# Two gates of the latent branch handed to the latent attention's filler, with that branch's products two gates behind

## The chip, the cores and the metric

The kernel runs on one core of a Trainium2 chip. A core has five engines that run their own queues in order and wait for each other through semaphores: TensorE (PE, with its weight loads PEld), VectorE (DVE), ScalarE (ACT), GpSimd (POOL) and SyncE (SP), whose queue issues the weight transfers here. The metric is the device time of one execution in microseconds (us), the median over several runs. One execution is taken by the hardware profiler, and all rows in the text come from it.

## What is computed

Two layers of an encoder trunk on 512 tokens of width 1024. In each layer, after one combined input projection of the normalised input, three branches are computed, each is projected to the model width, weighted by a sigmoid gate per token and channel, summed, and projected once more; a gated feed-forward with a short convolution follows. Cut to what matters here:

```
o_mla  = mla_branch(c_q, c_kv, k_rope, ...)      # 8 heads, latent attention
o_gqa  = gqa_branch(gq, gk, gv, ...)             # 8 heads, grouped queries
o_pool = pool_branch(pool_in, ...)
gates  = sigmoid(gate_logits)                    # 3 x 1024 channels, columns of h @ w_in
merged = gates[0] * (o_mla  @ w_branch_mla) + gates[1] * (o_gqa @ w_branch_gqa) \
       + gates[2] * (o_pool @ w_branch_pool)
x = x + merged @ w_out
x = x + (silu(u_gate) * u_val) @ ffn_w_down      # u: up-projection and width-3 convolution
```

The gate logits depend on the normalised input alone, the products `o @ w_branch` on the finished branch.

## The kernel before, in words

All work on TensorE is done with operands split into a high and a low part: `mm3` (L347) issues three matmuls of up to 512 columns for one product of 128 rows. Weights come from memory in order of use as one long stream of pieces; a piece is split into `wh` (ACT, L208) and `wl` (POOL or DVE, L215) shortly before its use, two pieces ahead, into four pairs of buffers.

The order of instructions on every engine is written while the kernel is built: the program keeps a clock of its own (`Clock`, L117) with a cost for each operation, and puts the follow-up steps of a matmul (`chain`, L167) into the engines' queues when that clock reaches them. On the chip the engines run these fixed queues and wait for semaphores.

Each of the three branches ends in `gates` (L804), a generator that yields unit by unit. A unit is one `mm3`, three matmuls. For each of the eight blocks m of 128 output channels there are two pieces of work:

- `gate(m)` (L806, called "g" in the order): 8 units that sum the gate logits over the eight blocks of the input; then `logits` on DVE multiplies them with the row norm into a tile `gt`, and ACT applies the tanh that makes the sigmoid.
- `branch(m)` (L819, "b"): 4 units that multiply the four head pairs of the branch (tiles `oh`, `ol`) with the branch weight; then `product` on DVE multiplies with the gate, `add` adds into the merged tile `XM`, and for the last of the three branches the sum is split into `mgh` (ACT) and `mgl` (DVE) and the residual is fetched back into `XM` by a transfer on SP.

`_order` (L57) says how the two are interleaved: g0 g1 b0 g2 b1 ... g7 b6 b7, so that b(m) comes one gate behind g(m). The same function orders the weight stream and its packing.

A `Filler` (L94) hands out such units one at a time. `attention` (L1026) lays its own steps on a plan of positions and before each step takes units from its filler: up to a target that rises evenly to the filler's total, and beyond it, up to 35 units, while the build-time clock says that the step would wait. A head of the latent attention consists of the transposes of queries and keys, four `s_max` products with a row maximum on DVE, `m_row` (one small matmul whose result DVE writes into four rows of `qa`), and for four key blocks k: `probs` (three matmuls into `ps_ST`, then on ACT the exponential and the copy `ph`, then on DVE the rest `pl`), `av_hi` (two matmuls that need `ph`) and `av_lo` (one that needs `pl`). After the last of a pair of heads `o_out` (L1192) copies sums and values (ACT, `osum` and `oraw`), takes four reciprocals (DVE, L235), multiplies and splits into `oh` and `ol`; for the last pair multiplication and `ol` are on DVE, for the others on POOL.

Branch 2 (pool) fills the grouped attention, branch 1 (grouped) fills the latent attention with 100 units, and branch 0 (latent) runs by itself behind the latent attention, since its products need that attention's heads. Then the output projection begins, whose every sum runs over all eight merged blocks.

Of the kernel before, what the change touches and what calls it, by code (L numbers as in the profile page):

```python
# [21 lines left out]
KC = D // P  # L22
# [34 lines left out]
def _order(br):  # L57


    r = []  # L60
    for m in range(KC + 1):
        r += [(k, pos.index(m)) for k, b, pos in EXTRA if b == br and m in pos]
        if m < KC:
            r.append(("g", m))
        if m > 0:
            r.append(("b", m - 1))
    return r


# [4 lines left out]
def _widths():  # L74

    r = [384] * KC + [T] * 8 + [T] * KC + [288] * 4 + [T] + [288] * 4
    for br in (2, 1, 0):
        for k, _ in _order(br):
            r += WIDTHS[k]
    return r + [T] * (2 * KC) + [T] * (4 * FC) + [T] * (2 * FC)  # L80
# [36 lines left out]
class Clock:  # L117
# [37 lines left out]
    def done(self, *key):  # L155
        self.ready[key] = self.fin + self.SEM

    def need(self, *keys):
        for k in keys:
            while k not in self.ready:  # L160
                self.pop()
            self.to(self.ready[k])
# [4 lines left out]
    def chain(self, *steps, after=0.2):  # L167

        def go(n, source=None):
            if n == len(steps):  # L170
                return
            keys, fn = steps[n] if isinstance(steps[n], tuple) else ((), steps[n])
            late = [self.ready.get(k, self.now + 0.5) for k in keys]
            if late and max(late) > self.now:
                self.at(max(late) - self.now, lambda: go(n))
                return
            self.fin, self.source, self.last = self.now, source, None
            fn()
            source, self.source = self.last, None
            self.at(max(0.0, self.fin - self.now), lambda: go(n + 1, source))  # L180
        self.at(after, lambda: go(0))
# [61 lines left out]
def trunk(ctx: ExitStack, tc: tile.TileContext, x, w, prm, gb, cst, out):  # L243
# [17 lines left out]
    def slot(name, dt=F32):  # L261
        uid[0] += 1
        t = sp.tile([P, SLOT], dt, tag="s", name=f"{name}_{uid[0]}")
        return t
# [9 lines left out]
    def ps(tag):  # L274
        while not banks[tag]:
            ck.pop()
        ck.to(heapq.heappop(banks[tag]))
        uid[0] += 1
        t = pp.tile([P, T], F32, tag=tag, name=f"ps_{tag}_{uid[0]}", bufs=nbank[tag])
        return t  # L280

    def free(tag):
        heapq.heappush(banks[tag], ck.fin + ck.SEM)
# [48 lines left out]
    def wnext():  # L332
        j = st["use"]
        w_ahead(j + st["la"] if j > LA else j)
        st["use"] += 1
        need(("w", j))
        return halves.pop(j)
# [9 lines left out]
    def mm3(o, lh, ll, rh, rl, start, stop):  # L347
        mm(o, lh, rh, start, False)
        mm(o, lh, rl, False, False)
        mm(o, ll, rh, False, stop)  # L350
# [19 lines left out]
    def split(hi, lo, src, scale=None, eng=None):  # L370

        steps = []
        if scale is None:
            steps.append(lambda: A.activation(hi, src, AF.Copy))
            steps.append(lambda: (eng or V).tensor_tensor(lo, src, f(hi), ALU.subtract))
        else:
            steps.append(lambda: A.activation(hi, src, AF.Copy, scale=scale))
            steps.append(lambda: V.scalar_tensor_tensor(lo, src, scale, f(hi), ALU.mult, ALU.subtract))
        return steps
# [120 lines left out]
    def layer(l, sq, xsrc):  # L500
# [48 lines left out]
        def feat_major(acc, gen):  # L549

            for kc in range(KC):
                if kc:
                    yield
                if kc % 4 == 0:
                    wh, wl = wnext()
                need(("H", gen, kc))
                ws = slice((kc % 4) * P, (kc % 4) * P + P)
                mm3(acc, wh[:, ws], wl[:, ws], HH[:, kc, :], HL[:, kc, :], kc == 0, kc == KC - 1)
# [245 lines left out]
        def gates(br, okey, odst, mode):  # L804
            hold = {}

            def gate(m):
                tag = "AV" if br == 2 and m < 2 else "acc"
                acc = ps(tag)
                yield from feat_major(acc, G1)  # L810
                t = hold[m] = slot("gt")

                def logits():
                    V.tensor_tensor(t[:, :T], acc, nrm["rbc"][:, :T], ALU.mult)
                    free(tag)

                chain(([("rbc", G1)], logits), lambda: A.activation(t[:, :T], t[:, :T], AF.Tanh, scale=0.5))

            def branch(m):  # L819
                acc = ps("acc")  # L820
                wh, wl = wnext()
                for kc in range(4):
                    if kc:
                        yield
                    need((okey, l, kc))
                    ws = slice(kc * P, kc * P + P)
                    oh, ol = odst[kc]
                    mm3(acc, wh[:, ws], wl[:, ws], oh[:, :T], ol[:, :T], kc == 0, kc == 3)
                t = hold.pop(m)

                def product():
                    dst = XM[:, m, :] if mode == "first" else t[:, :T]
                    V.scalar_tensor_tensor(dst, t[:, :T], 1.0, acc, ALU.add, ALU.mult)
                    free("acc")

                def add():
                    (V if mode == "last" else G).tensor_tensor(XM[:, m, :], XM[:, m, :], t[:, :T], ALU.add)

                def fin():
                    SY.dma_start(XM[:, m, :], xsrc[m])  # L840
                    done("mrg", l, m)

                if mode == "first":
                    chain(product)
                elif mode == "add":
                    chain(product, add)
                else:
                    mh, ml = slot("mgh", F32R), slot("mgl", F32R)
                    merged[m] = (mh, ml)
                    chain(product, add, *split(mh[:, :T], ml[:, :T], XM[:, m, :]), fin)  # L850

            extra = None
            for k, m in _order(br):
                if k in mla_make:
                    extra = mla_make[k](m)
                    continue
                work = branch(m) if k == "b" else gate(m)
                more = True
                while more:
                    if extra:  # L860
                        if next(extra, END) is END:
                            extra = None
                        yield
                    more = next(work, END) is not END
                    yield
# [395 lines left out]
        ogqa, omla = {}, {}  # L1261

        def units(br):
            return sum(UNITS[k] for k, _ in _order(br))
# [6 lines left out]
        while not ck.has(*[("gqn", l, b) for b in range(4)]) and fa.step():  # L1271
            pass
        attention("gqa", fa, "og", ogqa)
        fb = Filler(gates(1, "og", ogqa, "add"), units(1))
        fb.upto(PRE_B)
        while not ck.has(("mq", l, 0)) and fb.step():
            pass
        attention("mla", fb, "om", omla)
        Filler(gates(0, "om", omla, "last"), units(0)).finish()


        sq = slot("sq")
# [69 lines left out]
        last = l == L - 1  # L1352
# [45 lines left out]
    for l in range(L):  # L1398
        sq = layer(l, sq, x if l == 0 else xsp)
# [133 lines left out]
```

## Time and profile before

| what | us |
|---|---|
| median of 3 runs (lowest, highest) | 1684.97 (1683.23, 1685.66) |
| the profiled execution, its own time | 1685.89 |
| span of that execution, first to last instruction | 1684.1 |
| outside the span, by these two | 1.8 |

Stages of the first layer, by busy time of the engines in windows of the span (us):

| stage | window | PE | DVE | ACT | POOL |
|---|---|---|---|---|---|
| input projections, pool branch, norms | 0 to 118 | 104.43 | 89.47 | 54.51 | 54.79 |
| grouped attention, branch 2 as filler | 118 to 211 | 89.28 | 69.84 | 64.35 | 44.25 |
| latent attention, branch 1 as filler | 211 to 366 | 152.35 | 106.74 | 85.46 | 73.32 |
| branch 0 | 366 to 440 | 74.00 | 28.25 | 27.10 | 34.85 |
| output projection | 440 to 483 | 43.00 | 10.87 | 18.59 | 28.17 |
| feed-forward, up | 483 to 771 | 288.00 | 174.40 | 122.30 | 173.71 |
| feed-forward, down | 771 to 895 | 124.00 | 38.54 | 41.00 | 61.59 |

The second layer repeats this about 833 us later. The boundaries are rounded. A row of the timeline gives start and duration in us, engine, line, operation, output and inputs, shapes and count; in brackets the idle time of the engine just before it and what ended it. Matmuls are pipelined and their ends are modelled, so the time that a stretch of TensorE takes is read from the starts.

### The profile page before, as it was taken

How to read it: one execution, taken by the hardware profiler on the slowest of the kernel's cores; microseconds unless marked ns; L12 is line 12 of the kernel's file. 1: busy time of each engine (PE TensorE's matmuls, PEld its weight loads, DVE VectorE, ACT ScalarE, POOL GpSimd, SP SyncE). 2: the span in 40 equal slices, each digit the busy share in tenths (PEclk: the TensorE clock that was granted, in tenths of full speed). 3: DMA queues.
4: the chain of work that ended last, by engine and by line, in shares of the span. 5: the costliest groups of instructions: out<-in, count | busy, mean ns of one | idle time of the engine just before them, and what ended most of it. 6: DMA issues, size and time to landing. Idle time of an engine off the chain costs nothing.

```text
span 1684.1 us, 20306 instructions
## 1 busy us (share of the span) xinstructions
PE 1649.9 (98%) x7360; PEld 1332.9 (79%) x7360; DVE 952.3 (57%) x1542; ACT 773.0 (46%) x1364; POOL 885.1 (53%) x746
## 2 busy tenths in 40 slices
PE   8989999999999999999999999999999999999999
PEld 7777777778888888888887777777788888888887
DVE  7777767653356666630157777677533666766100
ACT  5356755553444444432334567455434444444221
POOL 4432763444566656655544427643446665666543
PEclk9999999999999999999999999999999999999999
DMA  5221121114323333233332211111133233232331
GB/s 173 79 85 50 51 72 52 39 53 127 110 87 99 90 99 96 91 109 116 99 108 79 82 45 60 60 51 51 59 128 102 87 100 100 89 100 88 112 119 56
DMA packets 44596, 145.40 MB, mean 86 GB/s; under 512 B 5072, under 2 KB 6352, under 8 KB 44496
## 3 DMA queue, kind: packets, MB, share of 16 engines
q1 hardware_dynamic: 44352, 144.10, 27.1%
q8 instruction: 58, 0.95, 0.3%
q14 instruction: 42, 0.34, 0.1%
q10 hardware_dynamic: 144, 0.01, 0.0%
HBM read 139.90 MB, written 4.19 MB: 86 GB/s over the span
## 4 chain that ended last, share of the span: by engine, by line
PE 88%; issue 5%; DVE 2%; ACT 2%; POOL 2%; DMA 1%; SPq 0%; POOLq 0%; ACTq 0%; DVEq 0%
PE ps_acc L340 40%; PE ps_ST L340 22%; PE ps_AV L340 22%; PE ps_S L340 2%; POOL wl L215 2%; PE ps_mi L344 1%; PE ps_mi L340 1%; ACT ps_ST L208 0%; DVE tabg L215 0%; ACT ph L208 0%; DMA raw<-w 0%; DMA prm<-prm 0%; DVE wl L215 0%; ACT qa L208 0%; ACT wh L208 0%
## 5 line engine op out<-in xcount | busy, mean ns | idle before, releaser
L215 POOL TENSOR_TENSOR wl<-raw,wh 128x512 fp32r<-128x512 f32 (+1 forms) x514 | 678.2, 1329 | 664.6 <-ACT wh L208 562.7
L208 ACT ACTIVATE wh<-raw 128x512 fp32r<-128x512 f32 (+3 forms) x522 | 314.8, 609 | 188.7 <-PE ps_ST L340 89.7
L219 DVE SCALAR_TENSOR_TENSOR a<-u,prm,a 128x512 f32<-128x512 f32 x176 | 240.1, 1365 | 79.5 <-ACT a L208 76.1
L340 PE MATMUL ps_acc<-HH,wh 128*128 128x512 f32 x592 | 234.6, 396 | 4.5 <-DVE XM L219 4.3
L340 PE MATMUL ps_acc<-HH,wl 128*128 128x512 f32 x592 | 233.9, 395 | 1.2 <-POOL wl L215 1.2
L340 PE MATMUL ps_acc<-HL,wh 128*128 128x512 f32 x592 | 233.7, 395 | 0.0
L340 PEld LDWEIGHTS ps_acc<-HH,wh 128*128 128x128 f32 x592 | 111.6, 189 | 31.2 <-ACT wh L208 5.7
L340 PEld LDWEIGHTS ps_acc<-HH,wl 128*128 128x128 f32 x592 | 111.5, 188 | 28.4 <-POOL wl L215 2.1
L340 PEld LDWEIGHTS ps_acc<-HL,wh 128*128 128x128 f32 x592 | 111.7, 189 | 25.2
L208 ACT ACTIVATE ps_ST<-ps_ST 128x512 f32<-128x512 f32 x128 | 74.5, 582 | 121.6 <-PE ps_ST L340 121.2
L340 PE MATMUL ps_AV<-HH,wh 128*128 128x512 f32 x288 | 113.9, 395 | 0.0
L340 PE MATMUL ps_AV<-HH,wl 128*128 128x512 f32 x288 | 113.7, 395 | 0.0
L340 PE MATMUL ps_AV<-HL,wh 128*128 128x512 f32 x288 | 113.7, 395 | 0.0
L223 DVE TENSOR_REDUCE nm<-ps_S 128x1 fp32r<-128x512 f32 x128 | 87.6, 684 | 44.4 <-PE ps_S L340 43.6
L215 POOL TENSOR_TENSOR al<-a,ah 128x512 fp32r<-128x512 f32 x44 | 58.2, 1323 | 84.8 <-ACT ah L208 56.5
L215 DVE TENSOR_TENSOR pl<-ps_ST,ph 128x512 fp32r<-128x512 f32 x128 | 87.1, 681 | 27.6 <-ACT ph L208 27.0
L340 PE MATMUL ps_ST<-HH,wh 128*128 128x512 f32 x240 | 94.9, 395 | 0.0
L340 PE MATMUL ps_ST<-HL,wh 128*128 128x512 f32 x240 | 94.8, 395 | 0.0
L340 PE MATMUL ps_ST<-HH,wl 128*128 128x512 f32 x240 | 94.7, 395 | 0.0
L208 ACT ACTIVATE a<-u,prm 128x512 f32<-128x512 f32 x88 | 71.9, 817 | 30.7 <-DVE u L215 30.7
L208 ACT ACTIVATE ah<-a 128x512 fp32r<-128x512 f32 x44 | 27.8, 632 | 116.3 <-DVE u L239 110.9
L208 ACT ACTIVATE a<-a 128x512 f32<-128x512 f32 x44 | 27.9, 633 | 114.0 <-DVE u L239 114.0
(343 smaller groups left out, 3542.3 us busy)
## 6 DMA issues: line engine op xcount, KB each, us to landing
raw<-w SPq DMA_DIRECT2D x228, 512.0 KB, 3.5
raw<-w SPq DMA_DIRECT2D x13, 384.0 KB, 3.1
XM<-x SPq DMA_DIRECT2D x16, 256.0 KB, 3.9
raw<-w SPq DMA_DIRECT2D x6, 448.0 KB, 3.3
xsp<-XM SPq DMA_DIRECT2D x8, 256.0 KB, 2.0
XM<-xsp SPq DMA_DIRECT2D x8, 256.0 KB, 3.1
out<-XM SPq DMA_DIRECT2D x8, 256.0 KB, 2.5
raw<-w SPq DMA_DIRECT2D x4, 432.0 KB, 3.2
```

What stands on the lines that cost most here:

```text
L208: return self.eng.activation(out, in_, func, **k)
L215: return self.eng.tensor_tensor(out, *a)
L219: return self.eng.scalar_tensor_tensor(out, *a)
L223: return self.eng.tensor_reduce(out, in_, *a, **k)
L340: PE.matmul(o, lhsT=lhsT, rhs=rhs, start=start, stop=stop)
L344: PE.transpose(o, src, ident)
```

## The change

`_order` gets a lag: two for branch 0, one for the others. For branch 0 the order becomes g0 g1 g2 b0 g3 b1 ... g7 b5 b6 b7. The filler of the latent attention becomes a generator that first hands out all 100 units of branch 1 and then 16 units of branch 0, its gates g0 and g1; its total is 116. What is left of branch 0 runs behind the attention, from wherever the generator stands.

```diff
-    r = []
-    for m in range(KC + 1):
+    r, lag = [], 2 if br == 0 else 1
+    for m in range(KC + lag):
         r += [(k, pos.index(m)) for k, b, pos in EXTRA if b == br and m in pos]
         if m < KC:
             r.append(("g", m))
-        if m > 0:
-            r.append(("b", m - 1))
+        if m >= lag:
+            r.append(("b", m - lag))
     return r
...
         attention("gqa", fa, "og", ogqa)
-        fb = Filler(gates(1, "og", ogqa, "add"), units(1))
+        fc = Filler(gates(0, "om", omla, "last"), units(0))
+
+        def beside():
+
+            yield from gates(1, "og", ogqa, "add")
+            for _ in range(2 * KC):
+                fc.step()
+                yield
+
+        fb = Filler(beside(), units(1) + 2 * KC)
         fb.upto(PRE_B)
         while not ck.has(("mq", l, 0)) and fb.step():
             pass
         attention("mla", fb, "om", omla)
-        Filler(gates(0, "om", omla, "last"), units(0)).finish()
+        fc.finish()
```

No instruction is added or removed; the same matmuls, splits and transfers stand in another order. On TensorE the order differs from the fifth head of the latent attention on to the end of branch 0, in each layer. Written with g and b for a filler unit, P for the three matmuls of `probs`, A for the two of `av_hi`, a for the one of `av_lo` and M for `m_row`, the end of the latent attention reads, from the last head's M on:

```
before: M Aa P Aa P Aa P Aa P Aa Aa g x16 b x4 g x8 b x4 ... g x8 b x8
after:  M Aa g P Aa P g Aa g P g A g a P g x2 Aa g x3 Aa g x11 b x4 g x8 ... g x8 b x12
```

## Prediction

> **What bounds the kernel now.** I read the page's head first, then the busy time by stage, then TensorE's waits in the stage that the change touches, then its timeline there.
>
> ```profile
> span 1684.1 us, 20306 instructions
> ...
> PE 1649.9 (98%) x7360; PEld 1332.9 (79%) x7360; DVE 952.3 (57%) x1542; ACT 773.0 (46%) x1364; POOL 885.1 (53%) x746
> ```
>
> TensorE is busy 98% of the span, so only idle time on TensorE can be won. The windows say where it is: the end of the latent attention, branch 0 alone, the feed-forward, and a short stretch of the second layer.
>
> ```profile
> 355.00:366.00 11.00, 9.40 (x35) 5.17 (x34) 4.62 (x7) 6.77 (x12) 5.54 (x6) 1.00 0.00 0
> 366.00:440.00 74.00, 74.00 (x321) 60.03 (x321) 28.25 (x39) 27.10 (x47) 34.85 (x27) 1.00 0.39 122
> 483.00:895.00 412.00, 412.00 (x1809) 335.80 (x1807) 212.95 (x351) 163.30 (x278) 235.30 (x175) 1.00 0.32 98
> 950.00:954.00 4.00, 3.71 (x13) 3.00 (x12) 1.53 (x3) 2.73 (x6) 0.36 (x1) 0.59 0.44 131
> ```
>
> Branch 0 has no idle time: 74.00 us for 321 matmuls, 0.231 us from start to start. The last 11 us of the attention hold 35 matmuls, which at that pitch are 8.1 us. The waits in that window:
>
> ```profile
> PE ps_AV L340 <- ACT ph L208: 1.3, 3, 0.6
> PE ps_ST L340 <- DVE qa L215: 0.3, 1, 0.3
> ```
>
> The last head has run out of filler, so TensorE stands still while ACT and DVE make `qa`, `ph` and `pl`. The starts show more than the waits:
>
> ```profile
> 355.55 0.22 PE L340 MATMUL ps_mi<-idr,nm 128*4 128x128 f32 x1
> ...
> 356.36 0.40 PE L340 MATMUL ps_ST<-qa,kl 96*128 96x512 f32 x1
> ...
> 357.30 0.47 PE L340 MATMUL ps_ST<-qa,kh 100*128 100x512 f32 x1 [0.31 <-DVE qa L215]
> ...
> 363.33 0.39 PE L340 MATMUL ps_ST<-qa,kh 100*128 100x512 f32 x1
> ...
> 365.03 0.50 PE L340 MATMUL ps_AV<-ph,vmh 128*128 128x512 f32 x1 [0.60 <-ACT ph L208]
> 365.37 0.39 PE L340 MATMUL ps_AV<-ph,vml 128*64 128x512 f32 x1
> 365.75 0.50 PE L340 MATMUL ps_AV<-pl,vmh 128*128 128x512 f32 x1
> 366.09 0.39 PE L340 MATMUL ps_acc<-HH,wh 128*128 128x512 f32 x1
> ```
>
> ```profile
> 1190.23 0.40 PE L340 MATMUL ps_ST<-qa,kl 96*128 96x512 f32 x1
> ...
> 1199.98 0.39 PE L340 MATMUL ps_acc<-HH,wh 128*128 128x512 f32 x1
> ```
>
> From the last head's first score matmul to the first gate matmul of branch 0 stand 27 matmuls (four P of three, five Aa of three). They take 366.09 - 356.36 = 9.73 us in the first layer and 1199.98 - 1190.23 = 9.75 in the second; at pitch 27 x 0.231 = 6.24. So 3.49 and 3.51 us are lost. The idle time in brackets is smaller because a matmul behind a stop takes 0.34 to its successor (365.03 to 365.37) and the stop ahead of `av_lo` carries no bracket (365.37 to 365.75 is 0.38).
>
> **The change part by part.** *The dealt-out gates.* No matmul is added. Of the 16 units of g0 and g1, three stand ahead of the last M, ten between it and the last `a`, three behind. Each moves 3 x 0.231 = 0.69 us of work from behind the stretch into it, and wins what TensorE would have idled there. I check each tile of the last head against what ACT and DVE need:
>
> ```profile
> 359.43 0.60 ACT L208 ACTIVATE osum<-ps_AV 64x512 f32<-64x512 f32 x1
> 360.04 0.59 ACT L208 ACTIVATE oraw<-ps_AV 64x512 f32<-64x512 f32 x1
> 360.54 0.58 ACT L208 ACTIVATE ps_ST<-ps_ST 128x512 f32<-128x512 f32 x1
> ...
> 363.76 0.58 ACT L208 ACTIVATE ps_ST<-ps_ST 128x512 f32<-128x512 f32 x1 [0.90 <-PE ps_ST L340]
> 364.38 0.60 ACT L208 ACTIVATE ph<-ps_ST 128x512 fp32r<-128x512 f32 x1
> 364.87 0.62 ACT L208 ACTIVATE wh<-raw 128x512 fp32r<-128x512 f32 x1
> ```
>
> ```profile
> 365.01 0.69 DVE L215 TENSOR_TENSOR pl<-ps_ST,ph 128x512 fp32r<-128x512 f32 x1 [1.42 <-ACT ph L208]
> 366.98 2.58 DVE L235 RECIPROCAL osum<-osum 128x128 f32<-128x128 f32 x3 [1.28 <-ACT osum L208]
> 371.89 0.69 DVE L215 TENSOR_TENSOR gt<-ps_acc,rbc 128x512 f32<-128x512 f32 x1 [2.33 <-PE ps_acc L340]
> 372.50 0.94 DVE L235 RECIPROCAL osum<-osum 128x128 f32<-128x128 f32 x1
> 373.54 0.69 DVE L215 TENSOR_TENSOR oraw<-oraw,osum 128x512 f32<-128x512 f32 x1
> 374.94 1.01 DVE L215 TENSOR_TENSOR ol<-oraw,oh 128x512 fp32r<-128x512 f32 x1 [0.70 <-ACT oh L208]
> ```
>
> Time 0 is the start of M; it takes 0.06, and every matmul behind it 0.231.
> - Rows of `qa`: from M to the third score matmul 357.30 - 355.55 = 1.75 are needed, with another DVE operation in front. The new order has eight matmuls between: third start at 0.06 + 8 x 0.231 = 1.91. Spare 0.16.
> - First tile: from the third score matmul to `av_hi` an undisturbed tile needs 365.03 - 363.33 = 1.70, to `av_lo` 365.75 - 363.33 = 2.42. The new order gives 10 x 0.231 = 2.31 and 12 x 0.231 = 2.77. Spare 0.61 and 0.35.
> - Second tile: on ACT it stands behind the first `ph` (which starts at 1.91 + 363.76 - 363.33 + 0.62 = 2.96), `osum` 0.62, `oraw` 0.61, and now a `wh` of 0.62 behind 0.50; its exponential starts at 5.31, its `ph` 0.62 later, its `av_hi` can start 0.65 after that (364.38 to 365.03): 6.58. The new order puts it at 0.06 + 30 x 0.231 = 6.99. Spare 0.41.
> - Third and fourth tile have 6 and 9 units' matmuls and more ahead of them.
>
> No tile waits, so all of 3.49 + 3.51 = 7.0 us goes. The spares are 0.16 to 0.6 us, no more; slipping by as much again would cost some tenths a layer. ACT gains three `wh` and a tanh in the stretch, about 4 x 0.62 = 2.5 us, and DVE one logits; ACT was busy 6.77 of 11, and behind M the ten units bring 6.9 us more matmuls. The bounds of this term are 0 and 7.0; the spares put it at 7.0.
>
> *The shorter cover behind the attention.* The copies, reciprocals and splits of the last head pair were hidden by 16 units of g0 and g1; g2 and three units are left, with three units of b0 ahead of the one that needs the pair. Counted from the first gate matmul (0 = 366.09): b0's first use of `ol` comes after 11 x 3 + 3 x 3 + 1 = 43 matmuls, at 9.93. In the new DVE queue stand: one reciprocal (366.98, 0.89), logits of g1 (a reader starts 0.43 behind the start of the last matmul, 363.33 to 363.76: 8 x 0.231 + 0.43 = 2.28 to 2.97), three reciprocals of 0.86 (2.58 / 3) to 5.6, the product of 0.69 to 6.3; ACT's `oh`, at the 0.62 of a `wh`, to 7.0; then logits of g2, which wait for g2's last matmul, 32 x 0.231 + 0.43 = 7.82 to 8.51; behind them `ol`, at 1.01 ready by 9.6. Spare 0.3, or 0.6 at 0.69. So the new wait of `ol` behind g2's logits costs nothing up to the 0.8 of the collision below, and I take nothing; without that cover every us of delay would be one us of TensorE.
>
> *The lag.* Blocks b5, b6, b7 come in a row, 12 matmuls = 2.77 us each; DVE has product, sum and split, 0.69 + 0.69 + 1.01 = 2.39 at most. The last block's split is ready 0.43 + 0.69 + 0.69 + 0.62 + 1.01 = 3.4 after b7's last matmul, and the output projection needs it 23 matmuls later, 5.3: nothing. Two more `gt` tiles are held; the order of the program has seven of 53 buffers free at its fullest, elsewhere.
>
> *Weights and DMA.* Four pieces, two transfers, move forward by the stretch:
>
> ```profile
> raw<-w SPq DMA_DIRECT2D x228, 512.0 KB, 3.5
> L215 POOL TENSOR_TENSOR wl<-raw,wh 128x512 fp32r<-128x512 f32 (+1 forms) x514 | 678.2, 1329 | 664.6 <-ACT wh L208 562.7
> ```
>
> They land in 3.5 us where DMA share is 0.00, on an SP queue that stays in stream order; the fetches of the residual behind them are wanted later. POOL has 4 x 1.33 us more and was busy 5.54 of 11. Nothing.
>
> **Sum.** 1684.1 - 7.0 = 1677.1 of span; with the 1.8 outside it 1678.9 for the profiled execution, which stood 0.9 above the median. Against the median: 1684.97 - 7.0 = 1678.0.
>
> **The rivals.**
> 1. *The second layer meets the clock otherwise.* The granted clock was 0.59 in 950 to 954: 4 x 0.41 = 1.6 us lost. The second layer now starts 3.5 us earlier; if the drop falls away 1676.4, if one more comes 1679.6. The Trainium skill (TensorE: Matmul & The Clock Gate, Part 1) says that the gate judges activity in a free-running window of 3.4 us, so that the same stop may or may not cost clock; the row agrees that a drop exists, and says nothing of phase.
> 2. *Waits move to ACT.* For: spares of 0.16 to 0.4. Against: they are all above zero by rows that include neighbours' delays. If half of the 7.0 stays: 1681.5.
> 3. *`ol` collides with a POOL split.* For: its row shows 1.01 against 0.69 beside this one:
>
> ```profile
> 373.85 3.24 POOL L215 TENSOR_TENSOR wl<-raw,wh 128x512 fp32r<-128x512 f32 x2 [2.98 <-ACT wh L208]
> ```
>
> If it waits out a whole split, 8.55 + 1.33 + 0.69 = 10.6 against 9.93: 0.8 with the restart, twice: 1679.6. Against: the next split's `wh` stands behind g2's tanh on ACT, so POOL should be free. The Trainium skill (SBUF — State Buffer, Who interferes with whom) lets the later of the two block for the whole instruction where VectorE reads two SBUF inputs and GpSimd reads SBUF; the 1.01 shows only part of that.
> 4. *Slower.* One place: b0's fourth unit. In the old DVE queue one reciprocal stood behind a gate's logits (2.33 idle, then 372.50). If all of this chain ran only behind g2's logits, it would end at 8.5 + 4 x 0.86 + 0.7 + 0.6 + 1.0 = 14.2, 4.3 late; with a clock drop behind it as in 950 to 954, 1.6, that is 5.9 a layer, 11.8 - 7.0 = +4.8: 1689.8. It makes the kernel slower once b0 stands still for more than 3.5 us a layer. Against: the new queue has only `ol` there, and the rest would have to slip by 7.8 - 7.0 = 0.8 first.
> 5. *It doesn't do what it says*, because the filler is used up earlier or full clock can't be held without pauses: 1685. Against: the order places ten units in the last head, and 412.00 of 412.00 us busy in the feed-forward went at clock 1.00.
>
> **How the numbers follow.** Chances: the forecast 1678.0, 0.57; clock better 0.13, worse 0.05; half stays 0.10; collision 0.05; nothing 0.05; slower 0.05. A change under 0.2% (3.4 us, 1681.6 to 1688.3) can't be told from none. Faster: 0.57 + 0.13 + 0.05 + 0.05 + half of rival 2 = 0.85; same 0.05 + 0.05 = 0.10; slower 0.05. The range reaches from rival 1's better end, 1676.2, to a little over rival 2, 1681.8.
>
> **What would show it.** Right: no bracketed wait on `ph` or `qa` in the last head, gate matmuls between its tiles, 27 matmuls of it and the dealt units at 0.231; no wait at b0's fourth unit; branch 0 and the output projection without gaps; second layer 3.5 us earlier, the end 7. Wrong: TensorE waiting for `ol` (DVE) behind g2, for `ph` behind a `wh` on ACT, or for `mgl` at the first output sum; or a lower clock where TensorE no longer pauses.

## The result, and the profile after

| | before | after |
|---|---|---|
| median of five runs (lowest, highest), us | 1684.97 (1683.23, 1685.66) | 1677.27 (1676.63, 1680.60) |
| the profiled execution, us | 1685.89 | 1680.60 |
| its span, us | 1684.1 | 1678.8 |

The ratio of the times is 0.9964, with a 95% interval of 0.9953 to 0.9974: 6.1 us of 1685, between 4.4 and 7.9; the two medians lie 7.7 apart. The forecast was 1678.0, a gain of 7.0.

The busy time by engine, from the head of the page after the change:

```profile
PE 1650.0 (98%) x7360; PEld 1336.1 (80%) x7360; DVE 949.4 (57%) x1542; ACT 774.0 (46%) x1364; POOL 886.6 (53%) x746
```

TensorE is as busy as before, 1650.0 against 1649.9, so what went is idle time on it. The busy time by window (time, PE, PEld, DVE, ACT, POOL, granted clock, DMA share, GB/s) says from where:

```profile
355.00:366.00 11.00, 11.00 (x49) 8.64 (x49) 3.95 (x6) 6.51 (x12) 7.04 (x6) 1.00 0.16 49
366.00:440.00 74.00, 74.00 (x321) 60.01 (x321) 30.18 (x42) 29.58 (x51) 34.16 (x27) 1.00 0.38 121
```

The window that held 35 matmuls and 9.40 us of work now holds 49 and 11.00; the one behind it stays full. The POOL splits (7.04 for 5.54) and the transfers (DMA share 0.16 for 0.00) have moved forward with the gates. In TensorE's timeline after the change, from the last head's M to the end of branch 0, no row carries a bracket, in either layer:

```profile
358.53 0.22 PE L340 MATMUL ps_mi<-idr,nm 128*4 128x128 f32 x1
...
360.02 0.40 PE L340 MATMUL ps_ST<-qa,kl 96*128 96x512 f32 x1
...
360.49 0.40 PE L340 MATMUL ps_ST<-qa,kh 100*128 100x512 f32 x1
...
362.83 0.39 PE L340 MATMUL ps_AV<-ph,vmh 128*128 128x512 f32 x1
...
363.29 0.39 PE L340 MATMUL ps_AV<-pl,vmh 128*128 128x512 f32 x1
...
365.60 0.39 PE L340 MATMUL ps_AV<-ph,vmh 128*128 128x512 f32 x1
...
372.55 0.39 PE L340 MATMUL ps_acc<-HH,wh 128*128 128x512 f32 x1
...
382.50 0.40 PE L340 MATMUL ps_acc<-ol,wh 128*128 128x512 f32 x1
...
1189.50 0.40 PE L340 MATMUL ps_ST<-qa,kl 96*128 96x512 f32 x1
...
1202.07 0.40 PE L340 MATMUL ps_acc<-HH,wh 128*128 128x512 f32 x1
```

From the last head's first score matmul to the first gate matmul behind its last `a` stand 54 matmuls, the 27 of the attention and nine dealt units. They take 372.55 - 360.02 = 12.53 us, 0.232 each, and 12.57 in the second layer. Before, the 27 alone took 9.73.

**Where the 5.3 us between the two spans came from.** The same matmul can be found in both traces: the first of the output projection, in the first and in the second layer. Before, then after:

```profile
432.81 0.39 PE L340 MATMUL ps_acc<-mgh,wh 128*128 128x512 f32 x1
...
1266.76 0.40 PE L340 MATMUL ps_acc<-mgh,wh 128*128 128x512 f32 x1
```

```profile
430.17 0.39 PE L340 MATMUL ps_acc<-mgh,wh 128*128 128x512 f32 x1
...
1259.97 0.39 PE L340 MATMUL ps_acc<-mgh,wh 128*128 128x512 f32 x1
```

The last head's first score matmul has four dealt units more ahead of it than before (three ahead of M, one behind), 12 x 0.231 = 2.77 us. Less these, it stands at 357.25 and 1186.73, where before it stood at 356.36 and 1190.23.

| stretch | gain, us |
|---|---|
| start to the last head, layer 1 | 356.36 - 357.25 = -0.89 |
| last head to output projection, layer 1 | 432.81 - 430.17 + 0.89 = 3.53 |
| from there to the last head, layer 2 | 757.42 - 756.56 = 0.86 |
| last head to output projection, layer 2 | 76.53 - 73.24 = 3.29 |
| from there to the end | 417.34 - 418.83 = -1.49 |

Here 757.42 and 756.56 are 1190.23 - 432.81 and 1186.73 - 430.17; 76.53 and 73.24 are 1266.76 - 1190.23 and 1259.97 - 1186.73. The changed stretches give 3.53 + 3.29 = 6.8. The rest, -1.5, lies where both kernels run the same order of work. The first two rests go largely with the clock. A drop is a stretch in which the granted clock reads 0.50; up to its last us the trace before has two, from 62.44 and 949.90 us, and the trace after four, from 17.57, 61.95, 116.56 and 922.11. One of before and one of after:

```profile
949.90:953.31 3.41, 3.41 (x13) 2.96 (x11) 1.38 (x2) 2.06 (x4) 0.46 (x1) 0.50 0.52 154
```

```profile
116.56:119.97 3.41, 3.41 (x12) 2.80 (x10) 1.38 (x2) 2.22 (x5) 0.39 (x1) 0.50 0.46 154
```

At 115 to 121 the clock of the trace before reads 1.00, at 948 to 954 that of the trace after. In the first layer one and the same matmul stands at 77.33 before and 77.49 after, a later one at 127.50 and 128.45: 0.8 of the 0.89 is lost around the drop at 116.56. In the second layer the drop follows the stop for `gqr` at 921 instead of the one for `XM` at 949, and the wait for `XM` that comes behind it is 0.90 instead of 2.11. In the last 418 us the clock reads 1.00 in both, and the 1.49 there are 0.4% of the matmul pitch; no row says why.

A drop of 3.41 us at half clock takes 0.001 off the mean clock of an execution of 1679 us, so the mean clock tells how many there were: 0.996 in the profiled execution is its four. That execution is 3.3 us above the median of its kernel; the other at 0.996 took 1680.36, those at 0.998 and 0.999 took 1676.63 to 1677.27.

### The profile page after: what moved, and what is told of

The parts are those of the page before. It is cut to its first block, busy times and chain, and to the rows that moved or that the text cites. A ratio compares the mean times of both kernels' runs of the same rounds, so it can differ in the third digit from the quotient of the medians.

```text
span 1678.8 us, 20300 instructions
## 1 busy us (share of the span) xinstructions
PE 1650.0 (98%) x7360; PEld 1336.1 (80%) x7360; DVE 949.4 (57%) x1542; ACT 774.0 (46%) x1364; POOL 886.6 (53%) x746
## 4 chain that ended last, share of the span: by engine, by line
PE 91%; issue 4%; DVE 2%; ACT 1%; POOL 1%; DMA 0%; SPq 0%; POOLq 0%; DVEq 0%; ACTq 0%
PE ps_acc L340 41%; PE ps_ST L340 23%; PE ps_AV L340 23%; PE ps_S L340 2%; PE ps_mi L340 1%; POOL wl L215 1%; PE ps_mi L344 1%; DMA XM<-x 0%; ACT qa L208 0%; ACT wh L208 0%; DVE vml L215 0%; DVE nm L223 0%; DVE gqr L215 0%; ACT ka L208 0%; DVE vmh L231 0%
```

## The experiments

Each diff is against the changed kernel. Ratios are against the kernel before on the same chip, medians of which were 1683.82 (first four) and 1684.55 (last three).

**lag_only: the lag without the dealing.** The order g0 g1 g2 b0 ... stays, but all of branch 0 runs behind the attention again.

```diff
-        fb = Filler(beside(), units(1) + 2 * KC)
+        fb = Filler(gates(1, "og", ogqa, "add"), units(1))
...
-        fc.finish()
+        Filler(gates(0, "om", omla, "last"), units(0)).finish()
```

> Only the lag: branch 0 runs wholly behind the latent attention, in the order g0 g1 g2 b0 g3 b1 ... b5 b6 b7; nothing is dealt into the attention. Theory (the 7 us come from the dealt units alone): the last head keeps its waits, 27 matmuls in 9.7 us instead of 6.2, and the time is that of the kernel before, 1685 within 1.5 us. Rival (the lag or the new order of branch 0 brings the gain, or part of it): 1678 to 1682, and the last head of the profile as before.

Measured: 1683.91, ratio 1.0003 (0.9994 to 1.0012). TensorE's waits in the window of the last head and the gates behind it, in total, times and longest:

```profile
PE ps_AV L340 <- ACT ph L208: 1.3, 3, 0.6
PE ps_ST L340 <- DVE qa L215: 0.3, 1, 0.3
```

These are word for word the waits of the kernel before, and there is none at b5, b6, b7 or the output projection. The lag by itself neither costs nor gains; the gain is the dealing's, and the next run shows that it needs the lag to be kept.

**deal2_lag1: the dealing without the lag.** Both gates are dealt out, and b0 comes right behind what is left of them.

```diff
-    r, lag = [], 2 if br == 0 else 1
+    r, lag = [], 1
```

> g0 and g1 are dealt out as in the changed kernel, but b0 follows g1 at once (lag one). Behind the last a stand three gate units, and b0's fourth unit follows after 9 + 9 matmuls, 4.2 us. Theory (g2 is there to cover the last pair's chain): by the queue orders and the rows of the changed profile the pair's oh is ready at about 7.0 us and ol at 7.7 after the first gate matmul, so TensorE waits about 2.9 us for oh and 0.5 for ol, 3.4 a layer, and a stop of that length may take the clock down for some us (up to 1.6): 1677.3 + 6.8 = 1684, up to 1687. The last head itself has no waits. Rival (the cover is not needed, the dealing alone is the gain): 1677 to 1678.

Measured: 1687.55, ratio 1.0023 (1.0014 to 1.0032): slower than before by 2.4 to 5.4 us. In its timelines of TensorE and DVE:

```profile
378.68 0.50 PE L340 MATMUL ps_acc<-oh,wh 128*128 128x512 f32 x1 [2.65 <-ACT oh L208]
379.40 0.50 PE L340 MATMUL ps_acc<-ol,wh 128*128 128x512 f32 x1 [0.22 <-DVE ol L215]
...
380.96 0.63 PE L340 MATMUL ps_acc<-HH,wh 128*128 128x512 f32 x1
381.39 0.63 PE L340 MATMUL ps_acc<-HL,wh 128*128 128x512 f32 x1
...
1213.42 0.80 PE L340 MATMUL ps_acc<-oh,wh 128*128 128x512 f32 x1 [2.63 <-ACT oh L208]
```

```profile
374.60 2.56 DVE L235 RECIPROCAL osum<-osum 128x128 f32<-128x128 f32 x3
377.27 0.69 DVE L215 TENSOR_TENSOR oraw<-oraw,osum 128x512 f32<-128x512 f32 x1
378.65 0.69 DVE L215 TENSOR_TENSOR ol<-oraw,oh 128x512 fp32r<-128x512 f32 x1 [0.69 <-ACT oh L208]
```

b0's fourth unit stands still while DVE works through the reciprocals, the product and, behind ACT's `oh`, the split `ol`. Start to start, the two waits lose 2.81 and 0.49 over the pitch, and then, in the first layer, seven matmuls run at 0.43 us instead of 0.23, 1.4 more. With the slower restarts the stretch from 375.63 to 383.86 loses 5.0; in the second layer, where part of the half clock falls into the wait, the one from 1210.39 to 1216.74 loses 4.5. That is 9.5 in all, some 4.7 a layer, against 7.0 gained: a loss of 2.5, the edge of the interval. The head's own waits are gone here too; the gain is made and more than given back. This is the place and the price of the slower rival, reached by leaving the lag out.

**deal1_lag2 and deal1_lag1: half of the dealing, with and without the lag.** Only g0 is dealt out.

```diff
-            for _ in range(2 * KC):
+            for _ in range(KC):
...
-        fb = Filler(beside(), units(1) + 2 * KC)
+        fb = Filler(beside(), units(1) + KC)
```

For deal1_lag1 the lag is 1 as well.

> Only g0 is dealt out (8 units instead of 16), lag two: g1 and g2 stand behind the attention. All 8 units fall between the last M and the last a. Theory (the last head can only use so much filler as its waits are long, 3.5 us or five units): nearly the whole gain, at most 0.3 us a layer left at the second tile, 1677.3 to 1678.5. Rival (the gain grows with the number of dealt units): half of it, 1681.

> Only g0 is dealt out, lag one: eight units of g1 stand behind the attention, then b0. Theory (queue order on DVE counts): the fourth reciprocal stands behind the logits of g1, which start 23 x 0.231 + 0.43 = 5.7 us after the first gate matmul; the chain behind it ends with oh at 8.8 and ol at 9.5, b0 needs them at 7.6 and 7.9: TensorE waits about 1.7 us a layer, 1677.3 + 3.4 = 1680.7. Rival (eight units, 5.5 us, are cover enough since the chain needs less): as with lag two, 1677.3 to 1678.5.

Measured: 1678.35 with the lag, ratio 0.9967 (0.9956 to 0.9978); 1680.88 without it, 0.9982 (0.9973 to 0.9991). With the lag no wait is left in the last head, so eight units fill it as well as sixteen do. Without it, the rows at b0's fourth unit:

```profile
375.47 0.50 PE L340 MATMUL ps_acc<-oh,wh 128*128 128x512 f32 x1 [1.03 <-ACT oh L208]
376.19 0.50 PE L340 MATMUL ps_acc<-ol,wh 128*128 128x512 f32 x1 [0.23 <-DVE ol L215]
376.53 0.39 PE L340 MATMUL ps_acc<-oh,wl 128*128 128x512 f32 x1
```

```profile
372.38 0.69 DVE L215 TENSOR_TENSOR gt<-ps_acc,rbc 128x512 f32<-128x512 f32 x1 [1.68 <-PE ps_acc L340]
372.99 0.94 DVE L235 RECIPROCAL osum<-osum 128x128 f32<-128x128 f32 x1
...
375.45 0.69 DVE L215 TENSOR_TENSOR ol<-oraw,oh 128x512 fp32r<-128x512 f32 x1 [0.69 <-ACT oh L208]
```

The queue explains the wait: the fourth reciprocal stands behind the logits of the one gate that is left, as it did before the change; DVE sits idle for 1.68 us waiting for that gate, and reciprocal, product, `oh` and `ol` run behind it. Idle and restart make 1.20 + 0.49 = 1.7 a layer over the pitch, 3.4 in all; the two medians differ by 2.5. In deal1_lag2 the same reciprocal also stands behind the logits of g1 (374.88, then 375.48, after 1.68 of idle time), but there the eight units of g2 follow, and TensorE waits for nothing. No half clock follows the stop of 1.03.

**deal3_lag3: one gate more.** Three gates dealt out, lag three.

```diff
-    r, lag = [], 2 if br == 0 else 1
+    r, lag = [], 3 if br == 0 else 1
...
-            for _ in range(2 * KC):
+            for _ in range(3 * KC):
...
-        fb = Filler(beside(), units(1) + 2 * KC)
+        fb = Filler(beside(), units(1) + 3 * KC)
```

> Three gates dealt out (24 units), lag three: g3 stands behind the attention, then b0. Theory (only the 3.5 us of waits a layer could be filled, and they are filled by now): no further gain, 1677 to 1679, ratio 0.996 to 0.997 of the kernel before, no waits in the last head and none at b0. Rival (every dealt gate brings about 1.75 us a layer, as 7 us for two gates in two layers would suggest): 1674.

Measured: 1677.86, ratio 0.9961 (0.9947 to 0.9974), no wait in the last head or at b0. Nothing is left there to win, and a longer lag costs nothing either.

**pool_late: what is left elsewhere.** Apart from 4.9 us at the start of the program, the largest waits on TensorE that remain lie in the input projections. In the changed kernel TensorE stops for the pool product, whose `ps_ST` bank DVE is still reading, and later for the first gate sum of branch 2:

```profile
90.51 0.50 PE L340 MATMUL ps_ST<-mxh,wh 128*128 128x512 f32 x1 [2.04 <-DVE gqr L215]
...
115.47 0.47 PE L340 MATMUL ps_acc<-HH,wh 128*128 128x512 f32 x1 [2.11 <-DVE XM L219]
```

The experiment moves that product, and its weight in the stream, from behind the fourth block of the key and value projection to behind the sixth.

```diff
-    r = [384] * KC + [T] * 8 + [T] * KC + [288] * 4 + [T] + [288] * 4
+    r = [384] * KC + [T] * 8 + [T] * KC + [288] * 6 + [T] + [288] * 2
...
-                if between and kc == 4:
+                if between and kc == 6:
...
-        res.insert(len(res) - 4, i["pool_w"][l].transpose(1, 0, 2).reshape(P, T))
+        res.insert(len(res) - 2, i["pool_w"][l].transpose(1, 0, 2).reshape(P, T))
```

> The changed kernel, and besides it the small product of the pool branch two of eight input blocks later in the projection of the grouped keys and values (its weights move in the stream with it). In the changed profile TensorE waits 2.0 us a layer ahead of this product for DVE (gqr, which frees the bank). The move puts 2 x 12 matmuls of 0.133 us, 3.2 us, ahead of it. Theory (TensorE sets the time everywhere, any wait of it that is covered comes back whole): 2.2 us a layer, 4.4 in all, 1673; less if what follows the product (its split, then branch 2) is late instead. Rival (the wait only moves on to the next user of DVE, which is busy there): 1677 to 1678, and the waits behind it longer by as much.

Measured: 1672.45, ratio 0.9930 (0.9918 to 0.9943), the fastest of all. The same stretch of its timeline:

```profile
106.52 0.66 PE L344 MATMUL ps_mi<-C,gk 128*128 128x128 f32 x4 [1.20 <-DVE gk L215]
...
111.95 0.47 PE L340 MATMUL ps_acc<-HH,wh 128*128 128x512 f32 x1 [0.92 <-DVE XM L219]
```

The wait of 2.04 is gone in both layers and one of 1.20 for `gk` stands in its place; the wait for `XM` is 0.92 and 0.91. For a comparison at one clock the profile of deal3_lag3 serves, from the same chip: it runs the changed kernel's order here, and like this one it has no drop in this stretch, in either layer. Its first layer:

```profile
88.61 0.50 PE L340 MATMUL ps_ST<-mxh,wh 128*128 128x512 f32 x1 [2.04 <-DVE gqr L215]
...
113.55 0.47 PE L340 MATMUL ps_acc<-HH,wh 128*128 128x512 f32 x1 [2.16 <-DVE XM L219]
```

Its second layer has 2.05 and 2.13, and the wait for `mqs` behind them is 0.94 or 0.95 in all four. The move takes 0.84 + 1.24 in the first layer and 0.85 + 1.22 in the second, 4.2 us, near the 4.4 that was expected: the wait moves on to `gk`, but not in full. The two medians on this chip, 1677.86 and 1672.45, differ by 5.4. The rest goes the way of the clock, 0.998 to 1.000 in these runs against 0.997 and 0.998, but the clock was not varied by itself.

**lag2_pool: the lag for the branch that fills the grouped attention.**

```diff
-    r, lag = [], 2 if br == 0 else 1
+    r, lag = [], 2 if br in (0, 2) else 1
```

> The changed kernel with the lag of two for the pool branch too, so that its b0 comes behind g2. In the changed profile TensorE waits 2.1 and 0.9 us (first and second layer) ahead of a gate of this branch for the product of b0 on DVE. Theory (the product then stands behind a gate that needs no such bank): about 2 us a layer less there, 1673 to 1675, unless the changed order of the grouped attention brings waits of its own. Rival (DVE is late anyway, and the next reader waits): no change, 1677 to 1678, or slower.

Measured: 1682.51, ratio 0.9989 (0.9980 to 0.9997), some 4 to 5 us slower than the changed kernel. The wait for `XM` is gone, and this stands ahead of it, in its timelines of TensorE and ACT:

```profile
113.17 0.44 PE L340 MATMUL ps_acc<-wh,cth 128*128 128x384 f32 x1 [1.90 <-ACT mqs L208]
```

```profile
109.54 2.41 ACT L208 ACTIVATE ka<-ps_mi 64x512 fp32r<-64x512 f32 x4
111.97 0.63 ACT L208 ACTIVATE gt<-gt 128x512 f32<-128x512 f32 x1
112.62 0.49 ACT L208 ACTIVATE mqs<-ps_acc 128x384 f32<-128x384 f32 x1
```

In the changed kernel the same four key copies and a tanh stand on ACT too, at 110.79 and 113.21, but TensorE meanwhile has the twelve matmuls of b0, from 109.25 to 112.13. With the lag these stand later, and TensorE reaches the reader of `mqs` while ACT is still at the copies. Other waits of the grouped attention follow (for `nm`, 0.99 and 1.45), and the one for `mns` shrinks from 1.5 to 0.3 and 0.4. TensorE's waits add up to 28.4 us in this profile and to 24.3 in that of the changed kernel. That each step's cover was already in use there, so that the lag only shifts units from one step to another, is my reading; no run separates it.

## Why the prediction was right, step by step

DVE and ACT after the change, in the last head and behind it:

```profile
358.78 0.68 DVE L215 TENSOR_TENSOR qa<-ps_mi,C 4x512 fp32r<-4x512 f32 x1 [1.34 <-PE ps_mi L340]
362.17 0.69 DVE L215 TENSOR_TENSOR pl<-ps_ST,ph 128x512 fp32r<-128x512 f32 x1 [2.70 <-ACT ph L208]
...
373.44 0.95 DVE L235 RECIPROCAL osum<-osum 128x128 f32<-128x128 f32 x1 [3.29 <-ACT osum L208]
374.83 0.69 DVE L215 TENSOR_TENSOR gt<-ps_acc,rbc 128x512 f32<-128x512 f32 x1 [0.44 <-PE ps_acc L340]
375.44 2.57 DVE L235 RECIPROCAL osum<-osum 128x128 f32<-128x128 f32 x3
378.11 0.69 DVE L215 TENSOR_TENSOR oraw<-oraw,osum 128x512 f32<-128x512 f32 x1
380.40 0.69 DVE L215 TENSOR_TENSOR gt<-ps_acc,rbc 128x512 f32<-128x512 f32 x1 [1.60 <-PE ps_acc L340]
381.01 0.68 DVE L215 TENSOR_TENSOR ol<-oraw,oh 128x512 fp32r<-128x512 f32 x1
```

```profile
361.54 0.60 ACT L208 ACTIVATE ph<-ps_ST 128x512 fp32r<-128x512 f32 x1
...
364.40 0.60 ACT L208 ACTIVATE ph<-ps_ST 128x512 fp32r<-128x512 f32 x1
...
378.83 0.63 ACT L208 ACTIVATE oh<-oraw 128x512 fp32r<-128x512 f32 x1 [0.76 <-DVE oraw L215]
```

- **The loss of 3.49 and 3.51 a layer, all of it won: held.** The trace gives 3.53 and 3.29, and no wait is left. The missing 0.2 is the pitch of the second layer, in branch 0 above all: from the first gate matmul behind the head to the output projection it takes 1259.97 - 1202.07 = 57.90 us, the first layer 430.17 - 372.55 = 57.62, for the same matmuls. That 1677.27 came within 0.8 of the forecast is partly luck: five runs spread over 4 us with the number of drops, and the two profiled executions lie 5.3 apart.
- **The spares of the tiles: held, one too tight.** A waiting matmul starts 0.05 behind the end of what it waits for (before, `ph` ended at 364.98 and `av_hi` started at 365.03). Less that, the first tile's `av_hi` has 362.83 - 362.14 - 0.05 = 0.64 (0.61 predicted), its `av_lo` 0.38 (0.35), the second tile 365.60 - 365.00 - 0.05 = 0.55 (0.41). The rows of `qa` have 360.49 - 359.46 - 0.05 = 0.98, not 0.16: the other DVE operation that I left ahead of `qa` is not there, DVE had been idle for 1.34.
- **The chain behind the attention: held.** Counted from the first gate matmul, logits of g1 start at 2.28 (2.28 predicted), the reciprocals end at 5.46 (5.6), the product at 6.25 (6.3), `oh` at 6.91 (7.0), logits of g2 start at 7.85 (7.82), and the matmul that needs `ol` starts at 9.95 (9.93). `ol` ends at 9.14, where 9.6, or 9.3 without a collision, was forecast: POOL was not in the way and it took 0.68. The spare is 0.8.
- **What the lag is worth: held.** With it the wait at b0 is zero; without it, 4.7 us a layer with two gates dealt and 1.7 with one. The claim that without cover one us of delay becomes one us of TensorE was too low for the long stop, which also cost clock.
- **Lag, weights, DMA at nothing: held**, the lag by lag_only's ratio of 1.0003, the other two by a branch 0 that stays busy for 74.00 of 74.00 us with weights and splits moved forward.
- **The rivals.** Half of the waits staying, the collision of `ol` and no effect are ruled out by the rows above. The slower one did not come about, but its place and its price are real: in deal2_lag1 b0's fourth unit stands still and the clock drops behind it, at 4.7 a layer where 5.9 was priced. The cause differs: there the chain does not run behind g2's logits, the cover is missing. The clock rival came about for part of the executions: where the drops fall differs, and that puts single runs up to 3.3 us above the median of 1677.27. The lower end of the range, 1676.2, was called rival 1's better end, which by its own sum is 1676.4; nothing hangs on it.

## What to carry to other kernels

Where an attention runs out of filler in its last head, the next stage's work that does not depend on it can be dealt in, but it was also the cover of the attention's own tail: count what the next dependent matmul has ahead of it, and put other independent work there (here by a lag) before taking the cover away. A step's place in an in-order queue counts, and not its length alone: one reciprocal behind a gate's logits cost 1.7 us a layer where that gate was the whole cover, and nothing with one more gate behind it. When a stretch has no wait left, as with one, two or three gates here, more of the same gains nothing, and the next largest wait in the list is the place to go.

## What the runs showed of the hardware

- The same stop does not always cost clock; it depends on where it falls. Up to the last 2 us of a trace every drop lasts 3.41 us at clock 0.50, and the drops of a trace start whole multiples of 3.413 us apart: in the changed kernel 13, 16 and 236 of them, between 17.57, 61.95, 116.56 and 922.11. Laid out on that grid, here is the stop of 2.04 or 2.03 us for `gqr`, first in the changed kernel, then in deal1_lag1, which runs the same order there:

```profile
85.84:89.25 3.41, 2.63 (x14) 1.89 (x12) 2.07 (x5) 2.12 (x4) 0.38 (x1) 1.00 0.10 38
89.25:92.66 3.41, 2.15 (x14) 2.02 (x15) 3.10 (x14) 1.30 (x3) 0.84 (x2) 1.00 0.34 124
```

```profile
85.22:88.63 3.41, 1.38 (x7) 0.81 (x5) 2.70 (x6) 2.36 (x4) 0.79 (x1) 1.00 0.00 0
88.64:92.05 3.41, 3.41 (x12) 3.12 (x13) 3.14 (x12) 1.02 (x2) 0.72 (x1) 0.50 0.50 156
```

  The second column is TensorE's busy time, and the rest of 3.41 is idle. In the first the edge at 89.25 splits the stop into 0.78 and 1.26 us, and the clock stays at 1.00, in the window behind as well. In the second the whole stop lies in one window, and the next runs at 0.50. With the grid taken from the drops, and 8 us at either end of a trace left out, the nine traces have 16 windows in which TensorE idles for 1.90 us or more, and a drop follows each; it follows 6 of the 14 with 1.55 to 1.87, and none with less.
- A drop nearly halves the rate: seven matmuls of 0.43 in deal2_lag1, behind its stop of 2.65. The Trainium skill (TensorE: Matmul & The Clock Gate, Part 1) describes a free-running window of 3.4 us and a clock that is either full or half; the grid and the pitch agree with that. The same section of the Trainium skill puts the fall to half clock at one idle window or more; here 1.90 us of idle time within one was followed by it each time.
- A matmul behind a stop takes 0.34 to its successor where 0.23 is usual (376.19 to 376.53 in deal1_lag1), so a wait costs 0.2 to 0.3 more than its bracket shows: 1.20 and 0.49 over the pitch for brackets of 1.03 and 0.23.
